# Conditioning sums of the first four k-tiles on TensorE, in a two-layer decoder

## The chip, the cores and the metric

The kernel runs on one core of one Trainium2 chip. The metric is the device time of one execution in microseconds (us). Before the change the median of 3 runs is 2377.34 us (2375.9 to 2378.76). The trace comes from one profiled execution of its own, which took 2369.32 us.

## The reference

Two decoder layers act on x (256 rows of 2048 features, float32). A condition c (2048 numbers) steers every sub-layer through six vectors per layer:

```
c_act = silu(c)
for l in range(2):
    mod = c_act @ w_ada[l] + b_ada[l]            # 2048 x 12288 weights per layer
    sh_a, sc_a, g_a, sh_m, sc_m, g_m = split(mod, 6)
    h = x * (1 + sc_a) + sh_a
    y = mixer(h, w_in[l], ..., w_o[l])           # attention, two kinds of heads
    x = layernorm(ALPHA * x + (1 + g_a) * y)
    h = x * (1 + sc_m) + sh_m
    y = square(relu(h @ w_up[l])) @ w_down[l]
    x = layernorm(ALPHA * x + (1 + g_m) * y)
```

All weights are read once from the chip's memory, as float32: w_ada alone is 2 x 100 MB. The change touches how the first part of `sc_a` and `sh_a` of layer 0 is made.

## The kernel before

The 2048 features lie in 16 k-tiles of 128 partitions. Every dense product splits its float32 operands into a rounded high part and the rest (`wh` and `wl` of the weights, two planes of `hT` for the activations) and multiplies three times: high by high, high by low, low by high (L302 to L304).

Weights stream in blocks of 512 KB into seven buffers with the tag `raw`, all issued from SyncE's queue (SP). A w_in block goes to ScalarE (ACT), which rounds it into `wh` (L134), then to VectorE (DVE), which subtracts to get `wl` (L135), then to TensorE (PE). A w_ada block (`rawa`) takes the same buffers and is summed on VectorE. A buffer is free for the next load when its last reader is done.

For 512 output features, that is four k-tiles, `ada_T` loads 16 blocks, one per k-tile of the condition: 128 rows of w_ada by 512 columns, for the shift vector and the scale vector together (128 x 1024 numbers). For each block VectorE does acc += block x (the condition's column of that k-tile), so that after 16 blocks each partition holds its own part of the sum. TensorE then transposes the eight 128 x 128 squares of `acc` (L166), VectorE adds each one up along its row (L171), adds the bias from `badaT` (L173), and the features lie on partitions in the two tiles called `mod`. Layer 0 begins with four passes over four k-tiles each (`PASSES`), and `first_pass` prepares each. For the first of them nothing else can run beside the sums: TensorE needs `hT`, which needs x transposed (L471) and scaled by the two `mod` tiles on ScalarE (L484), then split on VectorE (L486, L487).

The order of the work on each engine is fixed when the program is built, by the tile framework's scheduler, and an engine runs its list strictly in that order. `side`, `pending` and `later` are lists of work that the code interleaves with weight blocks.

One small place far from the change matters for reading the trace. In `forget`, once per layer, TensorE runs four plain float32 matmuls with 8 moving columns against a stationary tile of 128 columns:

```
for t in range(NT):
    for a in range(2):
        nc.tensor.matmul(pf[:, t * NF:(t + 1) * NF], lhsT=zr[:, a, t * P:(t + 1) * P],
                         rhs=sel[0:2 * NF, :], start=a == 0, stop=a == 1)   # line 715
```

Of the kernel before, what the change touches and what calls it, by code (L numbers as in the profile page):

```python
# [11 lines left out]
F32 = mybir.dt.float32  # L12
# [3 lines left out]
ALU = mybir.AluOpType  # L16
PSUM = bass.MemoryType.PSUM

P = 128
D = 2048  # L20
S = 256
NT = S // P
KT = D // P
# [14 lines left out]
CW = 512  # L38
# [5 lines left out]
RAW_BUFS = 7  # L44
# [29 lines left out]
def decoder(ctx: ExitStack, tc: tile.TileContext, x, c, positions, w_ada, b_ada, w_in, b_f,  # L74
            lambda_q1, lambda_k1, lambda_q2, lambda_k2, subln_g, w_o, ln1_g, ln1_b, w_up, w_down,
            ln2_g, ln2_b, out):
    nc = tc.nc
    const = ctx.enter_context(tc.tile_pool(name="const", bufs=1))
    big = ctx.enter_context(tc.tile_pool(name="big", bufs=1))
    wp = ctx.enter_context(tc.tile_pool(name="wp", bufs=1))  # L80
# [4 lines left out]
    def bank():  # L85
        return psum.tile([P, 512], F32, tag="bank", name="bank", bufs=4)
# [7 lines left out]
    def e1(shape, name, dtype=F32):  # L94
        return sm.tile(shape, dtype, tag="e1", name=name, bufs=E1_BUFS)
# [11 lines left out]
    cact = const.tile([P, KT], F32, name="cact")  # L107
# [8 lines left out]
    badaT = []  # L116

    def bias_T(l):
        r1 = e1([96, P], "r1")
        nc.sync.dma_start(r1, b_ada[l].rearrange("(a p) -> a p", p=P))  # L120
        pv = bank()
        nc.tensor.transpose(pv[:, 0:96], r1, ident[0:96, 0:96])
        bT = const.tile([P, 96], F32, name=f"badaT{l}")
        nc.vector.tensor_copy(bT, pv[:, 0:96])
        badaT.append(bT)


# [15 lines left out]
    def ada_add(acc, raw, kt, fresh):  # L143
        k = cact[:, kt:kt + 1]
        if fresh:
            nc.vector.tensor_scalar(acc, raw, k, None, ALU.mult)
        else:
            nc.vector.scalar_tensor_tensor(acc, raw, k, acc, ALU.mult, ALU.add)  # L148

    def ada_T(l, vec, kt0):  # L150

        acc = gp.tile([P, 2, CW], F32, tag="acc", name="acc", bufs=1)
        for kt in range(KT):
            raw = wp.tile([P, 2, CW], F32, tag="raw", name="rawa", bufs=RAW_BUFS)
            rows = w_ada[l, kt * P:(kt + 1) * P, :].rearrange("p (v n) -> p v n", n=D)
            nc.sync.dma_start(raw, rows[:, vec:vec + 2, kt0 * P:kt0 * P + CW])
            ada_add(acc, raw, kt, kt == 0)
            if kt < KT - 1:
                yield 1

        def finish():
            pss = []
            for i in range(2):
                ps = bank()
                for f in range(4):
                    nc.tensor.transpose(ps[:, f * P:(f + 1) * P], acc[:, i, f * P:(f + 1) * P], ident)  # L166
                pss.append(ps)
            yield
            for i, ps in enumerate(pss):
                red = sm.tile([P, 4], F32, tag="red", name="red")  # L170
                nc.vector.reduce_sum(red, ps.rearrange("p (f k) -> p f k", f=4), axis=mybir.AxisListType.X)  # L171
                s0 = (vec + i) * KT + kt0
                nc.vector.scalar_tensor_tensor(modT[l, vec + i][:, kt0:kt0 + 4], red, float(i),  # L173
                                               badaT[l][:, s0:s0 + 4], ALU.add, ALU.add)

        pending[(l, vec, kt0)] = [0, finish()]
        yield 1

    def ada_G(l, vec):
# [29 lines left out]
    modT = {}  # L209
    gates = {}  # L210
    ready = set()
    pending = {}
    side = []
# [5 lines left out]
    def want_mod(l, vec, kts=range(0, KT, 4)):  # L219
        for v in (vec, vec + 1):  # L220
            if (l, v) not in modT:
                modT[l, v] = const.tile([P, KT], F32, name=f"mod{l}_{v}")
        return [ada_T(l, vec, kt0) for kt0 in kts]

    def side_rate(per_block):
        rate[0] = per_block
# [12 lines left out]
    def side_pop():  # L239
        settle()  # L240
        try:
            return next(side[0])
        except StopIteration:
            side.pop(0)
            return 0
# [8 lines left out]
    def side_flush():  # L254
        while side:
            side_pop()
        settle(*pending)
# [110 lines left out]
    def masks():  # L368
        nc.gpsimd.memset(mhalf, -0.5)
        nc.gpsimd.memset(mask, 0.0)  # L370
        nc.gpsimd.affine_select(out=mask[:, 1, :], in_=mask[:, 1, :], compare_op=ALU.is_ge, fill=BIG,
                                base=0, pattern=[[-1, P]], channel_multiplier=1)
        nc.gpsimd.memset(tri, 1.0)
        nc.gpsimd.affine_select(out=tri[:, 0, :], in_=tri[:, 0, :], compare_op=ALU.is_ge, fill=0.0,
                                base=0, pattern=[[1, P]], channel_multiplier=-1)

        nc.gpsimd.memset(sel, 0.0)

        nc.gpsimd.memset(FL.bitcast(F32), 0.0)
        nc.gpsimd.memset(FG, 0.0)  # L380
        for i in range(4):
            nc.gpsimd.affine_select(out=sel, in_=sel, compare_op=ALU.not_equal, fill=1.0, base=-NF * i,
                                    pattern=[[-1, NF]], channel_multiplier=1)

        nc.gpsimd.memset(rowc, 1.0)
        for i in range(4):
            for base, sign in ((-NF * i, 1), (NF * (i + 1) - 1, -1)):
                nc.gpsimd.affine_select(out=rowc[:, i:i + 1], in_=rowc[:, i:i + 1], compare_op=ALU.is_ge,
                                        fill=0.0, base=base, pattern=[[0, 1]], channel_multiplier=sign)
        nc.gpsimd.affine_select(out=rowc[:, 4:5], in_=rowc[:, 4:5], compare_op=ALU.is_ge, fill=0.0,  # L390
                                base=-2 * NF, pattern=[[0, 1]], channel_multiplier=1)

    def constants():
# [58 lines left out]
        for l in range(DEPTH):  # L452
            nc.vector.tensor_scalar(neglam[:, l:l + 1], neglam[:, l:l + 1], -lambda_init(l), None, ALU.add)
            nc.vector.tensor_scalar(subg[:, l:l + 1], subg[:, l:l + 1], 1.0 - lambda_init(l), None, ALU.mult)
        bias_T(1)


    h_steps = [None, KT, KT]

    def need_h(upto):  # L460

        while h_steps[1] < min(upto, h_steps[2]):
            h_steps[1] = next(h_steps[0])
# [3 lines left out]
    def turn(k2):  # L467
        pt = bank().rearrange("p (a s) -> p a s", a=2)
        for j in range(2):
            for t in range(NT):  # L470
                nc.tensor.transpose(pt[:, j, t * P:(t + 1) * P],  # L471
                                    xacc[:, t, (k2 + j) * P:(k2 + j + 1) * P], ident)
        return pt

    def make_h(hT, A, B, kt0, kt1, coef=None):

        for k2 in range(kt0, kt1, 2):
            if coef is not None and k2 % 4 == 0:
                coef(k2)
            pt = turned.pop(k2) if k2 in turned else turn(k2)  # L480
            h32 = e2([P, 2, S], "h32")
            for j in range(2):
                kt = k2 + j
                nc.scalar.activation(h32[:, j, :], pt[:, j, :], AF.Identity,  # L484
                                     bias=B[:, kt:kt + 1], scale=A[:, kt:kt + 1])
            nc.vector.tensor_copy(hT[:, k2:k2 + 2, 0, :], h32)  # L486
            nc.vector.tensor_sub(hT[:, k2:k2 + 2, 1, :], h32, hT[:, k2:k2 + 2, 0, :].bitcast(F32))  # L487
            yield k2 + 2
# [524 lines left out]
    def x_rows(a, b):  # L1013
        for t in range(NT):
            nc.sync.dma_start(xacc[:, t, a * P:b * P], x[0, t * P:(t + 1) * P, a * P:b * P])
        yield (b - a) / 4

    def alpha_x(t, a, b):
        nc.scalar.mul(xacc[:, t, a * P:b * P], xacc[:, t, a * P:b * P], ALPHA)

    def first_pass(i):
        a, b = PASSES[i]
        if i == 0:
            side.extend(want_mod(0, 0, [a]))
            for _ in range(3):
                side_pop()
            for _ in x_rows(a, b):
                pass
            bias_T(0)
            masks()  # L1030
            for k2 in range(a, b, 2):
                turned[k2] = turn(k2)
        side_flush()
        h_steps[:] = [make_h(hT, modT[0, 1], modT[0, 0], a, b), a, b]
        need_h(a + AHEAD)
        for t in range(NT):
            later.extend([nop, nop, nop, nop, lambda t=t: alpha_x(t, a, b)])
        if i == 0:
            rest = constants()
            for _ in range(12):  # L1040
                later.append(lambda: next(rest, None))
        if i + 1 < len(PASSES):
            n = PASSES[i + 1]
            side.extend([x_rows(*n)] + want_mod(0, 0, [n[0]]))
            side_rate(4.5 * (n[1] - n[0]) / ((12 - SKIP) * (b - a) / 2))
        else:
            side.append(ada_G(0, 2))
            side.extend(want_mod(0, 3))

    for l in range(DEPTH):  # L1050
# [20 lines left out]
        else:  # L1071
            side.append(ada_G(l, 5))
            rows = []
# [30 lines left out]
```

## Time and profile before

| what | value |
|---|---|
| median of 3 runs | 2377.34 us |
| profiled execution | 2369.32 us |
| its span, first to last instruction | 2367.6 us |
| PE busy | 2281.3 us (96%) |
| DVE busy | 1790.1 us (76%) |
| ACT busy | 1155.3 us (49%) |
| moved by DMA | 619.37 MB, mean 262 GB/s |
| third dense matmul starts at | 38.16 us |

Times inside the trace count from the span's start; 1.7 us of the execution lie outside the span. A busy share is an average over stages. PE is nearly idle up to 37 us and nearly full from there on, so the two stretches are read apart. PE is the matmuls, PEld the loads of the stationary operand, which run beside the matmul before. The column of the granted clock reads 1.00 for all stretches before 41.7 us; durations of the rows themselves tell the level there.

### The profile page before, as it was taken

The page shows a single profiled execution, that of the slowest core. Times are in us where ns is not written, and L with a number is a line of the kernel's source. Part 1 is how long each engine was busy: PE and PEld are TensorE (multiplying, and loading weights), DVE is VectorE, ACT ScalarE, POOL GpSimd, SP SyncE. Part 2 cuts the span into 40 slices and gives each one's busy share as a digit, 9 for nine tenths or more (in the row PEclk, how much of TensorE's full clock was granted, in tenths as well). Part 3 has the DMA queues.
Part 4 walks back from the last instruction along what each step waited for, and adds up shares of the span by engine and source line. Part 5 has one row for each costly group of instructions (what it writes and reads, how often), then busy time and mean ns, then how long its engine had stood idle before and what let it go on. Part 6 is the DMA issues. An engine that isn't in the chain of part 4 may idle for free.

```text
span 2367.6 us, 33293 instructions
## 1 busy us (share of the span) xinstructions
PE 2281.3 (96%) x12444; PEld 1959.6 (83%) x12444; DVE 1790.1 (76%) x2339; ACT 1155.3 (49%) x1684; POOL 35.1 (1%) x60
## 2 busy tenths in 40 slices
PE   4999999899999999999999999999999999999998
PEld 3878798699989888888777778987888888888886
DVE  7899888988888778888777975667675666555657
ACT  2543675344546345346444663444554553553542
POOL 0000010000000000000000000000000000000000
PEclk9999999999999999999999999999999999999999
DMA  9999688889898888888759877765777777756653
GB/s 344 326 331 308 193 265 305 312 315 325 303 349 301 302 281 309 312 293 300 273 186 303 292 226 234 233 215 170 221 263 251 229 242 240 230 189 195 187 188 123
DMA packets 309890, 619.37 MB, mean 262 GB/s; under 512 B 24200, under 2 KB 25048, under 8 KB 309728
## 3 DMA queue, kind: packets, MB, share of 16 engines
q1 hardware_dynamic: 309728, 617.25, 77.6%
q8 instruction: 97, 1.59, 0.3%
q14 instruction: 65, 0.53, 0.1%
HBM read 615.07 MB, written 2.10 MB: 261 GB/s over the span
## 4 chain that ended last, share of the span: by engine, by line
PE 76%; DVE 9%; DMA 9%; issue 3%; ACT 2%; POOL 0%; SPq 0%; DVEq 0%; ACTq 0%; POOLq 0%
PE mm L303 13%; PE mm L302 13%; PE mm L304 13%; PE mm L908 7%; PE bank L908 7%; DMA rawa<-in_w_ada_dram 5%; PE mm L331 4%; PE mm L330 4%; PE mm L328 4%; PE mm L910 4%; PE bank L910 4%; DVE wl L135 4%; DVE acc L148 2%; DMA raw<-in_w_in_dram 1%; ACT wh L134 1%
## 5 line engine op out<-in xcount | busy, mean ns | idle before, releaser
L134 ACT CAST wh<-raw 128x1024 fp32r<-128x1024 f32 x752 | 789.5, 1052 | 929.5 <-PE mm L304 491.5
L135 DVE TENSOR_TENSOR wl<-raw,wh 128x1024 fp32r<-128x1024 f32 x752 | 913.7, 1221 | 347.2 <-ACT wh L134 343.9
L148 DVE SCALAR_TENSOR_TENSOR acc<-rawa,cact,acc 128x1024 f32<-128x1024 f32 x368 | 471.0, 1280 | 137.8 <-DMA rawa<-in_w_ada_dram 136.5
L303 PE MATMUL mm<-wl,Hs 128*128 128x512 f32 x992 | 386.5, 390 | 2.0 <-DVE wl L135 1.9
L302 PE MATMUL mm<-wh,Hs 128*128 128x512 f32 x992 | 386.2, 389 | 0.0
L304 PE MATMUL mm<-wh,Hs 128*128 128x512 f32 x992 | 386.0, 389 | 0.0
L331 PE MATMUL mm<-hT,wl 128*128 128x256 f32 x1024 | 289.6, 285 | 6.0 <-DVE wl L135 5.4
L328 PE MATMUL mm<-hT,wh 128*128 128x256 f32 x1024 | 290.9, 285 | 1.9 <-DVE hT L486 1.1
L330 PE MATMUL mm<-hT,wh 128*128 128x256 f32 x1024 | 289.8, 284 | 0.2 <-DVE hT L487 0.2
L908 PE MATMUL mm<-hT,wh 128*128 128x512 f32 x768 | 286.7, 396 | 0.5 <-DVE hT L487 0.5
L908 PE MATMUL bank<-hT,wh 128*128 128x512 f32 x768 | 286.2, 395 | 0.0
L303 PEld LDWEIGHTS mm<-wl,Hs 128*128 128x128 f32 x992 | 186.2, 188 | 41.9 <-DVE wl L135 3.5
L302 PEld LDWEIGHTS mm<-wh,Hs 128*128 128x128 f32 x992 | 186.2, 188 | 38.7
L304 PEld LDWEIGHTS mm<-wh,Hs 128*128 128x128 f32 x992 | 186.2, 188 | 38.6
L910 PE MATMUL mm<-hT,wl 128*128 128x256 f32 x768 | 215.5, 281 | 0.2 <-DVE wl L135 0.2
L910 PE MATMUL bank<-hT,wl 128*128 128x256 f32 x768 | 215.3, 280 | 0.0
L302 PE MATMUL mm<-wh,hT 128*128 128x512 f32 x512 | 200.8, 400 | 5.9 <-DVE hT L486 5.7
L303 PE MATMUL mm<-wl,hT 128*128 128x512 f32 x512 | 203.4, 397 | 3.1 <-DVE wl L135 2.7
L331 PEld LDWEIGHTS mm<-hT,wl 128*128 128x128 f32 x1024 | 196.0, 192 | 8.7 <-DVE wl L135 8.3
L304 PE MATMUL mm<-wh,hT 128*128 128x512 f32 x512 | 200.9, 393 | 0.0
L328 PEld LDWEIGHTS mm<-hT,wh 128*128 128x128 f32 x1024 | 196.8, 192 | 3.4 <-DVE hT L486 1.3
L330 PEld LDWEIGHTS mm<-hT,wh 128*128 128x128 f32 x1024 | 197.1, 192 | 0.8 <-DVE hT L487 0.4
(248 smaller groups left out, 2665.7 us busy)
## 6 DMA issues: line engine op xcount, KB each, us to landing
rawa<-in_w_ada_dram SPq DMA_DIRECT2D x384, 512.0 KB, 5.5
raw<-in_w_up_dram SPq DMA_DIRECT2D x256, 512.0 KB, 4.8
raw<-in_w_down_dram SPq DMA_DIRECT2D x256, 512.0 KB, 5.1
raw<-in_w_in_dram SPq DMA_DIRECT2D x192, 512.0 KB, 5.4
raw<-in_w_o_dram SPq DMA_DIRECT2D x64, 512.0 KB, 4.6
gb<-in_ln_g_dram SPq DMA_DIRECT2D x12, 256.0 KB, 5.5
bb<-in_ln_b_dram SPq DMA_DIRECT2D x12, 256.0 KB, 5.3
xacc<-in_x_dram SPq DMA_DIRECT2D x8, 256.0 KB, 6.7
```

The lines of the kernel that those rows point to most:

```text
L134: nc.scalar.copy(wh, raw)
L135: nc.vector.tensor_sub(wl, raw, wh.bitcast(F32))
L148: nc.vector.scalar_tensor_tensor(acc, raw, k, acc, ALU.mult, ALU.add)
L302: nc.tensor.matmul(o, lhsT=hi, rhs=wh, start=start, stop=False)
L303: nc.tensor.matmul(o, lhsT=hi, rhs=wl, start=False, stop=False)
L304: nc.tensor.matmul(o, lhsT=lo, rhs=wh, start=False, stop=stop)
L328: nc.tensor.matmul(o, lhsT=wh[:, j, cs], rhs=hT[:, kt, 0, :], start=first and kt == kt0 and f % 2 == 0, stop=False)
L330: nc.tensor.matmul(o, lhsT=wh[:, j, cs], rhs=hT[:, kt, 1, :], start=False, stop=False)
L331: nc.tensor.matmul(o, lhsT=wl[:, j, cs], rhs=hT[:, kt, 0, :], start=False, stop=last and kt == kt1 - 1 and f % 2 == 1)
L908: nc.tensor.matmul(pu[f], lhsT=wh[:, j, cs], rhs=hT[:, kt].rearrange("p a s -> p (a s)"), start=kt == kt0, stop=False)
L910: nc.tensor.matmul(pu[f][:, 0:S], lhsT=wl[:, j, cs], rhs=hT[:, kt, 0, :], start=False, stop=kt == kt1 - 1)
```

## The change

A new function `ada_start` takes the place of `ada_T` for the first four k-tiles of layer 0's shift and scale, and for those alone. It loads the same 16 blocks into the same seven buffers. Each 128 x 128 square of a block becomes the stationary operand of a matmul, with one column of the condition (`cact`) as the moving operand; eight such matmuls per block write eight columns of one accumulator bank, and 16 blocks add up there. The features come out on partitions, and VectorE adds the bias straight from the bank. The transposes, the row sums and VectorE's products of this part are gone. The bias is loaded, transposed and copied before the blocks, and its copy moves from VectorE to ScalarE, for both layers.

```diff
@@ bias_T
-        nc.vector.tensor_copy(bT, pv[:, 0:96])
+        nc.scalar.copy(bT, pv[:, 0:96])
@@
+    def ada_start(l, vec, kt0):
+
+        ps = bank()
+        for kt in range(KT):
+            raw = wp.tile([P, 2, CW], F32, tag="raw", name="rawa", bufs=RAW_BUFS)
+            rows = w_ada[l, kt * P:(kt + 1) * P, :].rearrange("p (v n) -> p v n", n=D)
+            nc.sync.dma_start(raw, rows[:, vec:vec + 2, kt0 * P:kt0 * P + CW])
+
+            for i in range(2):
+                for f in range(4):
+                    c = i * 4 + f
+                    nc.tensor.matmul(ps[:, c:c + 1], lhsT=raw[:, i, f * P:(f + 1) * P], rhs=cact[:, kt:kt + 1],
+                                     start=kt == 0 and c == 0, stop=kt == KT - 1 and c == 7)
+            if kt < KT - 1:
+                yield 1
+        for i in range(2):
+            s0 = (vec + i) * KT + kt0
+            nc.vector.scalar_tensor_tensor(modT[l, vec + i][:, kt0:kt0 + 4], ps[:, i * 4:i * 4 + 4], float(i),
+                                           badaT[l][:, s0:s0 + 4], ALU.add, ALU.add)
+        ready.add((l, vec, kt0))
+        yield 1
@@ first_pass
         if i == 0:
-            side.extend(want_mod(0, 0, [a]))
+            bias_T(0)
+            want_mod(0, 0, [])
+            side.append(ada_start(0, 0, a))
             for _ in range(3):
                 side_pop()
             for _ in x_rows(a, b):
                 pass
-            bias_T(0)
             masks()
```

The rows below give the order of instructions on an engine, without times; after the change the line numbers of the later code stand 22 higher (L302 becomes L324).

TensorE at the program's start, before: `ident,r` is the bias, `ident,xacc` are transposes of x, `ident,acc` those of the finished sums.

```order
L106 MATMUL bank<-ident,crow 128x16
L122 MATMUL bank<-ident,r_119 128x96
L471 MATMUL bank<-ident,xacc 128x128 x8
L166 MATMUL bank<-ident,acc 128x128 x8
L302 MATMUL mm<-wh,hT 128x512
L303 MATMUL mm<-wl,hT 128x512
L302 MATMUL mm<-wh,hT 128x512
L304 MATMUL mm<-wh,hT 128x512
```

The same place after the change:

```order
L106 MATMUL bank<-ident,crow 128x16
L122 MATMUL bank<-ident,r_105 128x96
L190 MATMUL bank<-cact,rawa 128x1 x24
L493 MATMUL bank<-ident,xacc 128x128 x8
L190 MATMUL bank<-cact,rawa 128x1 x104
L324 MATMUL mm<-wh,hT 128x512 x2
L325 MATMUL mm<-wl,hT 128x512
L326 MATMUL mm<-wh,hT 128x512
```

128 one-column matmuls (L190) stand on TensorE ahead of the first dense matmul, with x's transposes after the third block; two products with `wh` come before the first one with `wl`.

ScalarE up to the first results, before: `wh` is a w_in block's rounded part, `h` the scaled x, `dv` the first result.

```order
L108 ACTIVATE cact<-bank 128x16
L1019 ACTIVATE xacc<-xacc 128x512 x2
L134 CAST wh<-raw 128x1024 x2
L484 ACTIVATE h_222<-bank,mod_0_105,mod_1_106 128x256 x2
L484 ACTIVATE h_227<-bank,mod_0_105,mod_1_106 128x256 x2
L134 CAST wh<-raw 128x1024 x2
L798 COPY dv_272<-mm 128x512 x2
```

And after:

```order
L108 ACTIVATE cact<-bank 128x16
L124 COPY badaT_109<-bank 128x96
L1041 ACTIVATE xacc<-xacc 128x512 x2
L506 ACTIVATE h_320<-bank,mod_0_111,mod_1_112 128x256 x2
L506 ACTIVATE h_325<-bank,mod_0_111,mod_1_112 128x256 x2
L134 CAST wh<-raw 128x1024 x3
L820 COPY dv_370<-mm 128x512 x2
```

The bias copy came in, and the first two blocks' `wh` casts moved from ahead of the four `h` to behind them.

VectorE over the same stretch, before (`red` are the row sums):

```order
L146 TENSOR_SCALAR acc<-rawa,cact 128x1024
L124 COPY badaT_123<-bank 128x96
L148 SCALAR_TENSOR_TENSOR acc<-rawa,cact,acc 128x1024 x15
L171 TENSOR_REDUCE red<-bank 128x4
L135 TENSOR_TENSOR wl<-raw,wh 128x1024
L173 SCALAR_TENSOR_TENSOR mod_0_105<-red,badaT_123 128x4
L171 TENSOR_REDUCE red<-bank 128x4
L173 SCALAR_TENSOR_TENSOR mod_1_106<-red,badaT_123 128x4
L135 TENSOR_TENSOR wl<-raw,wh 128x1024
L486 CAST hT<-h_222 128x2x256
```

And after:

```order
L196 SCALAR_TENSOR_TENSOR mod_0_111<-bank,badaT_109 128x4
L196 SCALAR_TENSOR_TENSOR mod_1_112<-bank,badaT_109 128x4
L508 CAST hT<-h_320 128x2x256
L509 TENSOR_TENSOR hT<-h_320,hT 128x2x256
L508 CAST hT<-h_325 128x2x256
L509 TENSOR_TENSOR hT<-h_325,hT 128x2x256
L135 TENSOR_TENSOR wl<-raw,wh 128x1024 x2
L146 TENSOR_SCALAR acc<-rawa,cact 128x1024
```

The sixteen products and the bias copy are gone, and the first two `wl` moved from beside the bias adds to behind both pairs of `hT`.

## Rows read from the trace of the kernel before

**Rows 1.** The page: shares of the chain of waits, by engine.

```profile
PE 76%; DVE 9%; DMA 9%; issue 3%; ACT 2%; POOL 0%; SPq 0%; DVEq 0%; ACTq 0%; POOLq 0%
```

**Rows 2.** Waits of PE, 0 to 45 us: us in total, times, longest.

```profile
PE bank L166 <- DVE acc L148: 18.4, 1, 18.4
PE mm L302 <- DVE hT L486: 3.5, 1, 3.5
```

**Rows 3.** The chain in order of time: start, us, what.

```profile
3.93 7.23 DMA r<-in_b_ada_dram
```

**Rows 4.** Timeline of VectorE: start, us, engine, line, operation.

```profile
5.02 0.75 DVE L146 TENSOR_SCALAR acc<-rawa,cact 128x1024 f32<-128x1024 f32 x1 [3.93 <-DMA rawa<-in_w_ada_dram]
11.84 19.77 DVE L148 SCALAR_TENSOR_TENSOR acc<-rawa,cact,acc 128x1024 f32<-128x1024 f32 x15
...
33.48 1.22 DVE L135 TENSOR_TENSOR wl<-raw,wh 128x1024 fp32r<-128x1024 f32 x1
...
35.41 0.16 DVE L173 SCALAR_TENSOR_TENSOR mod<-red,badaT 128x4 f32<-128x4 f32 x1
...
36.66 0.43 DVE L486 CAST hT<-h 128x512 fp32r<-128x512 f32 x1
...
37.66 0.68 DVE L487 TENSOR_TENSOR hT<-h,hT 128x512 fp32r<-128x512 f32 x1
```

**Rows 5.** Timeline of PE, 0 to 39 us.

```profile
11.42 1.91 PE L471 MATMUL bank<-ident,xacc 128*128 128x128 f32 x8
31.75 1.94 PE L166 MATMUL bank<-ident,acc 128*128 128x128 f32 x8 [18.42 <-DVE acc L148]
37.14 0.79 PE L302 MATMUL mm<-wh,hT 128*128 128x512 f32 x1 [3.45 <-DVE hT L486]
...
38.16 0.63 PE L302 MATMUL mm<-wh,hT 128*128 128x512 f32 x1
```

**Rows 6.** Windows: engines' busy us (x instructions), granted clock, DMA share, GB/s.

```profile
11.84:31.70 19.86, 1.49 (x7) 1.09 (x6) 19.26 (x16) 2.19 (x3) 0.00 (x0) 1.00 1.05 389
...
41.70:97.00 55.30, 54.84 (x297) 47.41 (x295) 45.28 (x72) 29.63 (x41) 0.00 (x0) 1.00 0.98 336
```

**Rows 7.** Timeline of SP: issues of DMAs.

```profile
3.93 0.64 SPq L120 DMA_DIRECT2D r<-in_b_ada_dram  x1
```

**Rows 8.** Line 715, 230 to 236 us: duration ns min/median/max.

```profile
L715 PEld LDWEIGHTS bank<-sel,zr x8: 181/187/187, 234.1 to 234.9; 16*128 16x128 f32 x8
```

**Rows 9.** Timeline of PEld, the weight loads, at three places.

```profile
37.14 0.29 PEld L302 LDWEIGHTS mm<-wh,hT 128*128 128x128 f32 x1 [3.85 <-DVE hT L486]
...
234.14 0.96 PEld L715 LDWEIGHTS bank<-sel,zr 16*128 16x128 f32 x8 [0.35 <-issue]
235.12 0.19 PEld L302 LDWEIGHTS mm<-wh,hT 128*128 128x128 f32 x1
```

**Rows 10.** Windows where the granted clock changed; columns as in rows 6.

```profile
260.20:263.60 3.40, 2.47 (x12) 1.47 (x11) 3.40 (x9) 2.81 (x7) 0.00 (x0) 1.00 0.48 143
263.61:267.00 3.39, 3.39 (x9) 2.60 (x9) 3.38 (x20) 0.99 (x4) 0.00 (x0) 0.50 0.54 169
...
475.90:478.60 2.70, 2.69 (x13) 2.67 (x14) 2.30 (x7) 1.75 (x4) 0.00 (x0) 0.50 0.61 194
478.70:482.00 3.30, 3.30 (x29) 3.17 (x28) 3.29 (x9) 1.75 (x5) 0.00 (x0) 1.00 0.03 7
```

**Rows 11.** Timeline of PE within the half-clock stretch, and before it.

```profile
261.47 1.62 PE L648 MATMUL bank<-dkT,dqT 64*128 64x128 f32 x8
...
264.32 0.63 PE L304 MATMUL mm<-wh,hT 128*128 128x512 f32 x1
```

**Rows 12.** Timeline of ScalarE, 0 to 45 us.

```profile
13.15 1.15 ACT L1019 ACTIVATE xacc<-xacc 128x512 f32<-128x512 f32 x2 [10.11 <-PE bank L471]
30.39 1.04 ACT L134 CAST wh<-raw 128x1024 fp32r<-128x1024 f32 x1 [16.09 <-DMA raw<-in_w_in_dram]
...
35.61 1.93 ACT L484 ACTIVATE h<-bank,mod,mod 128x256 f32<-128x256 f32 x4 [1.46 <-DVE mod L173]
```

## The prediction

> **What bounds the kernel now.** I read the chain of waits first. TensorE holds 76% of it, VectorE and DMA 9% each [rows 1]; by place, PE is nearly full from 41.7 us on (54.84 of 55.30 us busy up to 97 us) [rows 6]. So what moves the start of the dense matmuls moves the end by about as much, unless work behind it has slack to give back.
>
> Then the waits of PE in the first 45 us. One wait of 18.4 us ends with VectorE's last product for `acc`, and one of 3.5 us with `hT` [rows 2]. Before the first, the chain goes through the bias: its DMA was issued behind three w_ada blocks and x, took 7.23 us and landed at 11.16 [rows 3]. Its copy stood on VectorE between the first product (5.02) and the other fifteen, which run from 11.84 for 19.77 us [rows 4], 1.32 us each. Over that stretch DMA delivers 389 GB/s [rows 6], which is 1.35 us for a block of 512 KB. Loads and VectorE are thus nearly in step. The reader is to see that two things pace this start, and that taking VectorE away leaves the loads: there is little to win beyond the late begin at 11.84.
>
> After the sums come eight transposes at 31.75 (1.94 us), row sums, and the second `mod` tile at 35.41 + 0.16 = 35.57. From there `h` takes 1.93 us on ScalarE for four [rows 12], `hT` follows, and the dense matmuls start at 37.14, the third at 38.16 [rows 5]. I use this third one as the marker, since it is the first that needs `wl` after the change.
>
> **The change part by part.** Removed: sixteen products on VectorE (0.75 + 19.77 us), eight transposes, two row sums. All stood on the path. VectorE has nothing else to do there, so their worth is only the path's.
>
> Added: 128 matmuls with one moving column, each with its own 128 x 128 float32 stationary square. The price is that of the loads of the stationary operand. The nearest rows are line 715: 8 moving columns, 128 stationary columns, plain float32. The code has four matmuls there per layer and the trace shows eight loads, so one such matmul runs as two records. The eight take 0.96 us, the last alone 0.187 [rows 8, 9], so one follows the other after (0.96 - 0.187) / 7 = 0.110 us. For 128 matmuls that makes 256 records, 28.3 us at this spacing; a block costs 16 x 0.110 = 1.77 us, more than VectorE's 1.32 or the load's 1.35. So PE, not the loads, would pace the start.
>
> That holds at full clock. At the start PE is not there: the third dense matmul lasts 0.63 us [rows 5], exactly as one at 264.32 [rows 11] in a stretch where the granted clock reads 0.50 [rows 10], the 1.2 GHz level. A first load took 0.29 us at 37.14 and 0.19 at 235.12 [rows 9], 0.10 more at the half level. I take 0.11 + 0.10 = 0.21 us per record there. The low bound for the half level is 0.11 (the load doesn't care), the high one 0.29 (each load stands alone, nothing overlaps). I choose 0.21, since the two loads differ only in the level.
>
> Does the stream of one-column matmuls lift the clock? No row shows one that long. What rows show: the clock rose just before 478.7 behind 14 loads and transposes that kept PE busy for 2.69 us. It fell at 263.6, behind a stretch in which PE was busy 2.47 of 3.40 us [rows 10], much of it eight matmuls on 64 of the 128 rows [rows 11]. So it has fallen behind work that occupied PE most of the time, and a one-column matmul sends less through the array than any row here. I take the half level for the whole stream, and keep the full level as a rival.
>
> The sum, on the trace's clock. The bias DMA now goes ahead of the blocks; its issue takes 0.64 us [rows 7], so the first block is usable at 5.02 + 0.64 = 5.66. Three blocks, 48 records: 10.1 us, to 15.7. Eight transposes of x queue behind them, 1.91 us [rows 5], to 17.6; x has landed by then, as the next blocks have. Thirteen blocks, 208 records: 43.7 us, to 61.3. Two bias adds of 0.16 us and the hand-over: `mod` at 61.7.
>
> Then an order that hurts. On ScalarE the `wh` casts now stand behind the four `h`, and on VectorE the `wl` behind both `hT` pairs. In the old order a `wh` cast was done at 31.4 [rows 12], long before. From `mod`: the first `hT` cast at +1.09 (36.66 - 35.57), then 0.43 + 0.68 twice, +3.3; `wh` is ready at 1.97 + 1.05 = +3.0; `wl` takes 1.22, +4.5 [rows 4, 12]. The third dense matmul starts at +4.55, against 38.16 - 35.57 = +2.59 before. That is 2 us lost, whatever the stream costs. Third matmul: 61.7 + 4.55 = 66.25, less 38.16 makes +28.1 us.
>
> Costed at nothing: the bias copy on ScalarE, which sat idle for 10.11 us there [rows 12] (about 0.3 us if that cover were gone); the slower loads while PE paces them, for the w_in blocks behind them land while PE is still loading squares. The seven buffers are now freed by PE, at 3.4 us per block, so DMA drops to some 156 GB/s in that stretch; it is not given back later, since at most seven blocks can wait ready. VectorE's freed 20 us lie where it would idle. The dense matmuls begin at the half level as before, so nothing there changes.
>
> The profiled execution, 2369.32 us, becomes 2397.4. The median of the runs shown lies 8 us higher; on that base I forecast 2377.3 + 28.1 = 2405.4 us.
>
> **The rivals.** First, the stream lifts the clock, and the change comes out even. For: PE is occupied without a gap, as in the 14 transposes that raised it. Then about 5 us run at the half level (24 records), 232 records at 0.110 take 25.6 us, the transposes some 1 us: end at 5.66 + 5 + 25.6 + 1 = 37.3, `mod` at 37.7, third matmul at 42.3, +4.1. The dense matmuls now start at full clock, which saves half of the 4.6 us up to 41.7 that ran at the half level, 2.3: +1.8 us, 2379.2. This is the other side, not slower: it decides if full clock is granted by about 12 us. The Trainium skill (TensorE: Matmul & The Clock Gate, Part 1) has the gate set by how busy the engine has recently been; by that rule as it stands this rival would hold. The fall at 263.6 with PE busy 2.47 of 3.40 us does not fit it well.
>
> Second, a load keeps its 0.11 us at either level. Then the end is 5.66 + 28.3 + 1.9 = 35.9, `mod` 36.3, third matmul 40.8: +2.7, 2380.0. For it speaks that line 715's spacing may be the feeding of instructions; against it the 0.29 beside the 0.19. The skill's same page (LDWEIGHTS) prices a load at its columns over 1.2 GHz, 107 ns for 128, and names no level: the 0.110 at full clock agrees, the 0.29 does not, and by the page the 256 records would cost 27.3 us, an estimate.
>
> Third, faster: with one column instead of eight a record costs less than 1.35 / 16 = 0.085 us, and the loads pace the start. The last block lands at about 5.66 + 15 x 1.35 + 1.35 for x = 27.3; with `mod` near 28.6 and the 4.55 behind it the third matmul starts at 33.2, -5.0 us: 2372.4, or 2370 if the clock is up too. Against: a record's load has 128 columns however few move.
>
> Fourth, worse: at the half level load and matmul don't overlap, 0.29 per record, 256 x 0.08 = 20 us on top: 2426.
>
> **How the numbers follow.** Forecast 0.61, first rival 0.19, second 0.08, third 0.08, fourth 0.04. The forecast's own range is 2400 to 2412: 3 us for the spacing (0.20 to 0.22) and 3 for the order behind `mod` and the drift of the base. The whole range takes in the first two rivals, 2376 to 2412; the third and fourth, about 0.12, lie outside. About 0.2%, 4.8 us, is what a measurement of this kernel can tell from no change. The first two rivals lie inside it except for their tails: same 0.26; faster 0.09 from the third; slower 0.65.
>
> **What would show it.** In the changed profile the one-column matmuls (line 190) should come as 256 records from about 5.7 us, spaced 0.21 us, ending near 61, with the first full granted clock only after the dense matmuls have run some 4 us. PE's wait for VectorE's `acc` is gone; the third dense matmul waits for `wl` near 66 us; the rest of the trace is the old one, moved by 28 us. Spacing of 0.11 after the first 5 us means the first rival, 0.11 from the first record the second, waits on w_ada loads between the blocks the third, 0.29 the fourth. I am also wrong if the later passes, which wait for sums that VectorE still makes, give back several us.

## The result and the profile after

The changed kernel takes 2401.33 us (median of 4 runs, 2397.56 to 2407.11), the kernel before in the same sitting 2376.62 us (4 runs, 2374.53 to 2378.76). The ratio is 1.0114 [1.0082, 1.0146]: slower by 19 to 35 us. The profiled execution is the one of 2407.11 us, with a span of 2405.4.

The chain of waits, shares by engine, looks the same as in [rows 1], with DMA and VectorE in the other order:

```profile
PE 76%; DMA 9%; DVE 9%; issue 3%; ACT 2%; POOL 0%; DVEq 0%; SPq 0%; ACTq 0%; POOLq 0%
```

A total over 2400 us hides a change in the first 60. The line of the one-column matmuls shows it: duration in ns (min/median/max), first and last start in us.

```profile
L190 PEld LDWEIGHTS bank<-cact,rawa x256: 289/333/338, 5.5 to 61.4; 128*128 128x128 f32 x128
L190 PE MATMUL bank<-cact,rawa x256: 212/352/353, 5.5 to 61.5; 128*128 128x1 f32 x128
```

The 128 matmuls run as 256 records (rows of the trace), and the shortest load lasts 289 ns. [rows 9] showed both prices of a first load, 0.29 us before the clock came up and 0.19 at full clock; here not one of 256 shows the lower. The timeline of PE answers [rows 5]: start and length in us, operation, count, and in brackets the wait ahead.

```profile
5.51 10.38 PE L190 MATMUL bank<-cact,rawa 128*128 128x1 f32 x48 [1.90 <-DMA rawa<-in_w_ada_dram]
15.75 1.95 PE L493 MATMUL bank<-ident,xacc 128*128 128x128 f32 x8
17.49 44.37 PE L190 MATMUL bank<-cact,rawa 128*128 128x1 f32 x208
65.17 1.22 PE L324 MATMUL mm<-wh,hT 128*128 128x512 f32 x2 [3.31 <-ACT wh L134]
66.71 0.79 PE L325 MATMUL mm<-wl,hT 128*128 128x512 f32 x1 [0.32 <-DVE wl L135]
...
71.14 0.63 PE L324 MATMUL mm<-wh,hT 128*128 128x512 f32 x1
...
72.12 0.39 PE L324 MATMUL mm<-wh,hT 128*128 128x512 f32 x1
```

208 records in 44.37 us is 0.213 us each, nearly twice the 0.110 worked out from [rows 8, 9]. PE waits for nothing from 17.49 to 61.86. The dense matmuls drop from 0.63 to 0.39 us only at about 71.6: up to there PE is at the 1.2 GHz level. The third dense matmul starts at 66.71 against 38.16: its offset, how much later than before it starts, is 28.55 us.

VectorE and ScalarE after the sums, to set beside [rows 4, 12]:

```profile
61.98 0.23 DVE L196 SCALAR_TENSOR_TENSOR mod<-bank,badaT 128x4 f32<-128x4 f32 x2 [60.89 <-PE bank L190]
...
64.82 0.69 DVE L509 TENSOR_TENSOR hT<-h,hT 128x512 fp32r<-128x512 f32 x1
65.43 2.35 DVE L135 TENSOR_TENSOR wl<-raw,wh 128x1024 fp32r<-128x1024 f32 x2
```

```profile
62.25 1.93 ACT L506 ACTIVATE h<-bank,mod,mod 128x256 f32<-128x256 f32 x4 [43.58 <-DVE mod L196]
64.06 2.94 ACT L134 CAST wh<-raw 128x1024 fp32r<-128x1024 f32 x3
```

`mod` is there at 62.21 and the third dense matmul 4.50 us later; it was 2.59 before. The casts stand behind the four `h`, so the first dense wait is for ScalarE's `wh` (3.31 us), and `wl` comes behind both `hT` pairs.

Two windows of the stream (columns as in [rows 6]), one early and one after the buffers were full:

```profile
6.00:16.00 10.00, 10.00 (x49) 10.00 (x49) 0.00 (x0) 0.00 (x0) 0.00 (x0) 1.00 1.01 353
20.00:41.00 21.00, 21.00 (x100) 21.00 (x100) 0.00 (x0) 0.00 (x0) 0.00 (x0) 1.00 0.48 151
```

PE is busy for all of both stretches, and DMA falls from 353 to 151 GB/s once PE, which frees the buffers, sets the pace. The granted-clock column reads 1.00 until the first change that was recorded; the level is told here by the loads, none shorter than 0.289 us, and by the dense matmuls of 0.63 us behind them.

Two more us arise later. VectorE's small operations on positions stand among the `wl` there, and PE waits:

```profile
96.26 0.61 PE L324 MATMUL mm<-wh,hT 128*128 128x512 f32 x2
97.16 0.50 PE L325 MATMUL mm<-wl,hT 128*128 128x512 f32 x1 [0.29 <-DVE wl L135]
...
99.58 0.61 PE L324 MATMUL mm<-wh,hT 128*128 128x512 f32 x2
101.15 0.50 PE L325 MATMUL mm<-wl,hT 128*128 128x512 f32 x1 [0.96 <-DVE wl L135]
```

In the kernel before no `wl` is waited for there, though the same operations stand among its `wl` from 62 to 70 us. What differs as well is ScalarE's order. Before, four `wh` casts stand ahead of the first two copies of results (`dv`), after the change three, so the fourth cast comes behind copies that wait for PE. The first two rows are from the kernel before, the others from the changed one:

```profile
42.36 1.05 ACT L134 CAST wh<-raw 128x1024 fp32r<-128x1024 f32 x1 [3.89 <-PE mm L304]
44.36 0.59 ACT L798 COPY dv<-mm 128x512 f32<-128x512 f32 x1 [0.95 <-PE mm L304]
...
73.70 1.27 ACT L820 COPY dv<-mm 128x512 f32<-128x512 f32 x2 [6.70 <-PE mm L326]
74.86 2.00 ACT L134 CAST wh<-raw 128x1024 fp32r<-128x1024 f32 x2
```

The fourth cast starts 32.5 us later than before, where PE's matmuls are 29.4 later. The second marker, the first `hT` matmul of the next pass, is at 129.13 against 97.59: +31.5 us. From there to 260 us the offset stays within 0.1 us; further on it grows, with steps back of 1 to 2 us, to 37.8 at the end.

### The profile page after: what moved, and what is told of

Read it like the earlier page. It is cut to its first block, busy times and chain, and to the rows that moved or that the text cites. A ratio compares the mean times of both kernels' runs of the same rounds, so it can differ in the third digit from the quotient of the medians.

```text
span 2405.4 us, 33757 instructions
## 1 busy us (share of the span) xinstructions
PE 2338.9 (97%) x12692; PEld 2015.0 (84%) x12692; DVE 1769.2 (74%) x2319; ACT 1155.3 (48%) x1686; POOL 35.3 (1%) x60
## 4 chain that ended last, share of the span: by engine, by line
PE 76%; DMA 9%; DVE 9%; issue 3%; ACT 2%; POOL 0%; DVEq 0%; SPq 0%; ACTq 0%; POOLq 0%
PE mm L325 13%; PE mm L326 13%; PE mm L324 13%; PE mm L930 7%; PE bank L930 7%; DMA rawa<-in_w_ada_dram 6%; PE mm L353 4%; PE mm L350 4%; PE mm L352 4%; DVE wl L135 4%; PE mm L932 3%; PE bank L932 3%; PE bank L190 2%; DVE acc L148 2%; ACT wh L134 1%
## 5 line engine op out<-in xcount | busy, mean ns | idle before, releaser
L148 DVE SCALAR_TENSOR_TENSOR acc<-rawa,cact,acc 128x1024 f32<-128x1024 f32 x353 | 451.8, 1280 | 157.0 <-DMA rawa<-in_w_ada_dram 156.0
L324 PE MATMUL mm<-wh,Hs 128*128 128x512 f32 x992 | 386.2, 389 | 0.0
L324 PEld LDWEIGHTS mm<-wh,Hs 128*128 128x128 f32 x992 | 186.2, 188 | 38.8
L324 PE MATMUL mm<-wh,hT 128*128 128x512 f32 x512 | 200.1, 402 | 5.6 <-ACT wh L134 3.3
```

The lines of the kernel that those rows point to most:

```text
L324: nc.tensor.matmul(o, lhsT=hi, rhs=wh, start=start, stop=False)
```

## The experiments

Two measures recur: the third dense matmul ("third", 38.16 before, 66.71 after) and the start of the next pass ("pass", 97.59 and 129.13). The kernel before had a median of 2373.26 us (20 runs) beside the first four experiments, 2372.28 (29 runs) beside the next four, and ranged from 2366.82 to 2379.93. Edits are against the changed kernel, save for experiment 2.

**1. The changed kernel again.** No edit; is the loss of the first 66 us kept to the end?

> The changed kernel once more, unedited, in five rounds, to size the change. My theory (256 records at the half level, 2 us of order behind the bias adds, 2 us of VectorE's lag) says the shift is made before 105 us and carried whole: +24 to +32 us over the kernel before, third dense matmul again near 66.7 us. If the later stages give time back (rival), the traced offset against the kernel before shrinks after 250 us and the median shows under +22.

2402.14 us (2400.58 to 2407.88), ratio 1.0122 [1.0101, 1.0143], +24 to +34 us. Pass is at 128.92, and at 2302 us of the before trace the same matmuls are 31.2 us late. Between, the offset went up to 35 and back. Nothing is given back; the two profiled executions of one kernel differ by 6.5 us at the end (2400.58, 2407.11), so a later offset of that size is no effect of the change.

**2. Only the move of the bias.** The kernel before, with its sums on VectorE; the bias is loaded and turned first.

```diff
-        nc.vector.tensor_copy(bT, pv[:, 0:96])
+        nc.scalar.copy(bT, pv[:, 0:96])
...
+            bias_T(0)
             side.extend(want_mod(0, 0, [a]))
...
-            bias_T(0)
```

> The kernel before with one part of the change alone: the bias is loaded, transposed and copied (on ScalarE) ahead of the blocks; the sums stay on VectorE. Theory: VectorE's fifteen products no longer wait for the copy from 5.8 to 11.8 us and follow the loads, the last block landing near 28; the sums end near 29 to 30 instead of 31.6 and the third dense matmul starts 2 to 3 us earlier, at 35 to 36: 2374 us, 0.1% faster, hardly to be told from no change. Rival, that the loads and not the copy already set the end: third matmul at 38, no difference in the trace.

2373.92 us, ratio 1.0003 [0.9989, 1.0017]. Third is at 36.78, 1.4 us earlier where 2 to 3 were expected, because VectorE no longer waits for the bias but for a block that was queued behind x:

```profile
12.68 1.28 DVE L148 SCALAR_TENSOR_TENSOR acc<-rawa,cact,acc 128x1024 f32<-128x1024 f32 x1 [2.72 <-DMA rawa<-in_w_ada_dram]
```

So the move of the bias costs nothing that shows, and the loss belongs to the sums on PE and to the order that the program has with them. It also shows how little VectorE could have freed: without its late begin, the loads are next.

**3. 64 moving columns.** The condition's column is repeated 64 times by a stride of zero: the same loads, more columns behind each.

```diff
-                    nc.tensor.matmul(ps[:, c:c + 1], lhsT=raw[:, i, f * P:(f + 1) * P], rhs=cact[:, kt:kt + 1],
+                    nc.tensor.matmul(ps[:, c * 64:c * 64 + 64], lhsT=raw[:, i, f * P:(f + 1) * P],
+                                     rhs=cact[:, kt:kt + 1].broadcast_to([P, 64]),
...
```

> The changed kernel with the condition's column repeated 64 times as the moving operand: the same 256 loads of stationary squares, 64 columns through the array for each instead of 1. Theory, that the cost is the half clock and one column does not lift it: the granted clock rises within some 10 us of the stream's start, spacing falls from 0.21 to 0.11 us, the stream ends near 37 instead of 61.9, the third dense matmul starts near 42: 2376 to 2381 us, within 0.2% of before. Rival, that the spacing is the load's and the feeding's own price: spacing stays at 0.21, end near 62, 2400 us as after the change.

The nine times fall into two groups: 2377.11, 2381.52, 2385.43, 2385.53 and 2399.57, 2399.79, 2402.91, 2403.52, 2408.25. A median (2399.57, ratio 1.0089 [1.0058, 1.012]) says little of such a pair. The traced execution was of the first group:

```profile
20.00:41.00 21.00, 21.00 (x191) 21.00 (x190) 0.00 (x0) 0.00 (x0) 0.00 (x0) 1.00 0.84 276
```

190 loads in 21 us are 0.110 each, against 100 in the same window of after. The rate changed at 19.3 us, just behind x's eight transposes; third is 46.78, where 42 was expected. What the other group does was seen later (9 and 10).

**4. Casts ahead.** One column; the first two blocks of w_in are loaded and split before the last four w_ada blocks, so that `wh` and `wl` don't stand behind `h` and `hT`.

```diff
+            if kt == KT - 4:
+                for kb in (0, 2):
+                    ahead.append(wload(rows_of(w_in[0])(kb, 2, OFF_DV, CW), 2, CW))
...
```

> The changed kernel with the first two w_in blocks loaded before the last four w_ada blocks, so that their splits (wh on ScalarE, wl on VectorE) stand ahead of the scaled x on both engines. Theory: the third dense matmul starts 2.4 to 2.6 us behind the bias adds instead of 4.5, and VectorE, two wl earlier, no longer makes TensorE wait near 97 and 101 us (1.25 us there): 3 to 4 us less than after the change, about +21 to +25 over the kernel before. Rival, that the order costs nothing because VectorE's lag moves elsewhere: the offset at 105 us stays at 31 us.

2399.0 us (2396.07 to 2401.67), ratio 1.0104 [1.0083, 1.0124], +20 to +29 us. The first and third dense matmul:

```profile
63.78 0.79 PE L331 MATMUL mm<-wh,hT 128*128 128x512 f32 x1 [1.84 <-DVE hT L515]
...
64.80 0.63 PE L331 MATMUL mm<-wh,hT 128*128 128x512 f32 x1
```

Third is 1.9 us earlier than in the first trace of the changed kernel, 2.6 behind `mod`, as in the kernel before; pass is 126.22, 2.7 earlier than in experiment 1. So the order behind `mod` cost about 2 us; the other 26.6 us of third's offset stand with the stream. The expectation that the later waits for `wl` go with it was wrong: 1.2 us of them stay, and ScalarE still has three casts ahead of the first copies.

**5. 128 moving columns.** As 3, with 128 columns and two banks.

```diff
-        ps = bank()
+        ps = [bank(), bank()]
...
-                    nc.tensor.matmul(ps[:, c:c + 1], lhsT=raw[:, i, f * P:(f + 1) * P], rhs=cact[:, kt:kt + 1],
+                    nc.tensor.matmul(ps[i][:, f * P:(f + 1) * P], lhsT=raw[:, i, f * P:(f + 1) * P],
+                                     rhs=cact[:, kt:kt + 1].broadcast_to([P, P]),
...
```

> The changed kernel with the condition's column repeated 128 times (two accumulator banks). With 64 columns the clock rose in some executions, right behind the transposes of x, and in others the time was that of one column. Theory: with 128 columns the stream lifts the clock by itself in every execution, by some 13 us; spacing 0.21 before and 0.11 after; stream ends at 37 to 39, third dense matmul at 42 to 44; the time is 2377 to 2383 us in all executions. Rival, that it was the transposes alone that lifted it: the rise comes only behind them, at about 19 us, or not at all, and the times fall in two groups again.

2376.45 us (10 runs, 2369.78 to 2379.66, one group, its median just below the 2377 to 2383 expected), ratio 1.0009 [0.9998, 1.002]. Three stretches of the stream:

```profile
5.80:11.00 5.20, 5.20 (x24) 5.20 (x25) 0.00 (x0) 0.00 (x0) 0.00 (x0) 1.00 0.98 291
11.30:13.80 2.50, 2.50 (x24) 2.50 (x24) 0.00 (x0) 0.00 (x0) 0.00 (x0) 1.00 1.04 393
14.80:37.80 23.00, 23.00 (x208) 23.00 (x207) 3.45 (x7) 3.22 (x4) 0.00 (x0) 1.00 1.00 350
```

25 loads in 5.20 us, then 24 in 2.50: the level changed near 11.2 us, ahead of any transpose of x, and stayed to the stream's end. This is the change with nothing taken off PE's work (columns were added to every matmul), and nearly all of the loss is gone. What is left shows at the end of the stream:

```profile
14.69 23.39 PE L190 MATMUL bank<-cact,rawa 128*128 128x128 f32 x208
42.63 0.80 PE L326 MATMUL mm<-wh,hT 128*128 128x512 f32 x1 [4.56 <-DVE hT L510]
...
43.66 0.63 PE L326 MATMUL mm<-wh,hT 128*128 128x512 f32 x1
```

PE waits 4.56 us, the dense matmuls are back at the half level (0.63), and third is 5.5 us later than before. In VectorE's order position operations and a `wl` stand ahead of the two bias adds or between them (39.55 and 40.89, where the sums ended at 38.1). ScalarE has four casts ahead of the first copies here, and PE has none of the later waits for `wl`.

**6. A warm start.** One column as in the changed kernel, behind 16 matmuls of ones, 512 columns each, that count for nothing in the output.

```diff
+            warm = mm()
+            for n in range(16):
+                nc.tensor.matmul(warm, lhsT=ones_r, rhs=ones_r.unsqueeze(1).broadcast_to([P, 4, P]),
+                                 start=n == 0, stop=n == 15)
             bias_T(0)
```

> The changed kernel with 16 matmuls of 512 columns (ones times ones, result unused) ahead of the stream, so that it begins at full clock; the stream starts near 8.7 us instead of 5.5. Theory, that one column does not hold the clock: after at most a few us at 0.11 the spacing goes to 0.21 and stays; end at 60 to 64, third dense matmul at 65 to 68, 2398 to 2404 us. Rival, that one column can hold what it cannot raise: spacing 0.11 throughout, end near 38, third matmul near 43, 2378 us.

2405.84 us (2403.08 to 2412.38), 2 us above the range expected, ratio 1.0144 [1.0128, 1.0161]. The stream begins at 7.88 us, at full clock:

```profile
7.90:9.50 1.60, 1.60 (x15) 1.60 (x15) 0.00 (x0) 0.21 (x1) 0.00 (x0) 1.00 1.01 257
9.70:15.00 5.30, 5.30 (x27) 5.30 (x26) 0.00 (x0) 0.00 (x0) 0.00 (x0) 0.50 1.03 381
20.00:60.00 40.00, 40.00 (x190) 40.00 (x189) 0.00 (x0) 0.00 (x0) 0.00 (x0) 0.50 0.49 158
```

This is the clearest row of the study. The same instruction goes at 0.11 us per load up to 9.5 and at 0.20 behind the recorded fall of the granted clock at 9.6, and DMA delivers more in the second stretch than in the first, so the squares (the 128 x 128 weights) were not late. And PE is busy 40.00 of 40.00 us at a granted 0.50. The stream does not merely fail to raise the clock, it lets it fall.

**7. 128 columns and casts ahead,** the edits of 4 and 5 together.

> 128 columns and the first two w_in blocks' splits ahead, both remedies on the changed kernel: stream's end as with 128 columns alone, third dense matmul 2 us earlier, at 40 to 42, no waits of TensorE for wl near 75 us: 2374 to 2379 us, not told from the kernel before. If it stays at or above 2381 us, there is a third cost that I have not named.

2377.35 us (12 runs), ratio 1.0016 [1.0006, 1.0027], not told from experiment 5 (1.0009 [0.9998, 1.002]). Against the kernel before it is slower by 1.4 to 6.4 us, where no difference was expected. Third is 42.35, 1.3 us earlier than in 5, just behind the 40 to 42 expected: a third `wl` still stands ahead of the bias adds at 39.53. As in 5, four casts stand ahead of the first copies and PE has none of the later waits for `wl`, though the operations on positions do stand among the `wl` here; pass is 102.52 against 103.92.

**8. Half and half.** VectorE sums the shift half of each block, PE the scale half with 128 columns; the bias first.

```diff
...
+                nc.vector.scalar_tensor_tensor(acc, raw[:, 0, :], cact[:, kt:kt + 1], acc, ALU.mult, ALU.add)
+            for f in range(4):
+                nc.tensor.matmul(ps[:, f * P:(f + 1) * P], lhsT=raw[:, 1, f * P:(f + 1) * P],
+                                 rhs=cact[:, kt:kt + 1].broadcast_to([P, P]),
...
```

> A version meant to beat both: of each w_ada block VectorE sums the shift half (512 columns, about 0.65 us) while TensorE sums the scale half with 128 repeated columns (0.9 us at full clock), both under the 1.35 us that a block's load takes; bias first. Theory, loads now pace the start: last block near 28, bias adds done near 30.5, third dense matmul at 33 to 34 instead of 38.2, of which the bias-first run suggests that a third is lost again in the first pass: 2368 to 2372 us, 0.1 to 0.3% faster. Rival, that the first pass is bound by loads and VectorE anyway: the traced offset shrinks to under 2 us by 105 us and the time is that of before.

2369.76 us (12 runs, 2367.41 to 2373.78), ratio 0.999 [0.9981, 0.9999]: the best of the study, 0.2 to 4.5 us faster than the kernel before and so only just told from no change. PE near the end of the sums:

```profile
29.92 1.16 PE L193 MATMUL bank<-cact,rawa 128*128 128x128 f32 x8 [0.20 <-DMA rawa<-in_w_ada_dram]
...
34.01 0.50 PE L335 MATMUL mm<-wh,hT 128*128 128x512 f32 x1 [2.50 <-DVE hT L519]
...
34.58 0.40 PE L335 MATMUL mm<-wh,hT 128*128 128x512 f32 x1
```

PE now waits for each block's load, as VectorE does. Third is 3.6 us earlier than before (34.58, where 33 to 34 was expected). With both engines waiting for loads, a faster sum on the same loads has little more to win. By pass (96.12) 1.5 us are left of it, since the waits for `wl` of 1.2 us come here too (three casts ahead of the first copies).

**9 and 10. 64 columns, two more executions** of kernel 3, unedited.

> 64 repeated columns once more, for a trace of the other group of times. Theory: where the time is near 2400 us the granted clock has not risen behind the transposes of x, the spacing is 0.21 us to the stream's end near 62 us; where it is near 2380 us the rise is at 16 to 20 us and the spacing 0.11 behind it. Rival: both groups have the same start, and the 20 us between them come later.

> The same as the run before, a third trace: either group, with the spacing of its group.

2411.29 and 2406.28 us, one run each (the kernel before beside them 2369.35). Both are of the second group. In experiment 9:

```profile
20.00:41.00 21.00, 21.00 (x101) 21.00 (x100) 0.00 (x0) 0.00 (x0) 0.00 (x0) 1.00 0.47 150
```

100 loads where the traced execution of 3 had 190, in the same window of the same program; the rate never changed, and in experiment 10 neither (208 records in 44.48 us in both). So, as far as these three traces show, the two groups of times are with and without the rise of the clock.

## Why the prediction was right

The forecast was slower, 2405.4 us or +28.1; 2401.33 was measured, +24.7, and +28.9 in experiment 1. Some of that closeness is luck, since the trace has +31.5 by the second pass. Each step against its row:

- **The price of a load, 0.21 us at the half level.** 0.213 measured. The 0.10 by which a lone load lasts longer at the half level was added to the spacing at full clock, which no row had tested; twice the spacing, 0.22, fits nearly as well, so it is partly luck. The bounds, 0.11 and 0.29, are both out as a spacing; 0.29 to 0.33 is what a load record lasts, but two of them overlap. The second rival (0.11 at either level) and the fourth (0.29) fall with it. Experiment 6 shows both prices in one stream. The Trainium skill (TensorE: Matmul & The Clock Gate, LDWEIGHTS) puts a load at its columns over 1.2 GHz, 107 ns for 128 as an estimate: that fits the full level (23.39 / 208 = 0.112 us in experiment 5) and not the half level.
- **The stream leaves the clock at the half level.** It does, for all of 56 us, and experiment 6 shows it lets a full clock go. The argument, that one column sends little through the array, is borne out in direction: more columns behind the same loads brought the clock up, sometimes with 64 and in every run with 128 as far as times and traces show. The Trainium skill (the same page, Part 1) sets the gate by how busy the engine has recently been. By the row at a granted 0.50 with PE busy 40.00 of 40.00 us, busy as the profile counts it is not what decides here. The first rival, at 0.19, falls. Its price was about right where its condition was made to hold: it put the third dense matmul at 42.3 and experiment 5 has 43.66. It is luck in part: the second bias add came 3.3 us later than that rival had it, at 41.04, and third stood 2.6 behind it in place of 4.55. It had the dense matmuls start at full clock, and they started at the half level, behind a wait of 4.56 us.
- **The start and the end of the stream.** First block 5.66 forecast, 5.51 measured; end 61.3 and 61.86; `mod` 61.7 and 62.21. The half microsecond is about what 208 records at 3 ns more come to.
- **The order behind `mod`.** +4.55 forecast, +4.50 measured; experiment 4 takes 1.9 us of it back by moving the casts alone.
- **The loads.** 156 GB/s forecast while PE paces them, 151 measured, and PE waits for no w_in block's load right behind it. The third rival, loads pacing the start, needs less than 0.085 us per record, and no row of any run shows that with 16 per block. With half the squares on PE, in experiment 8, it does hold.
- **What was costed at nothing and was not.** "The dense matmuls begin at the half level as before, so nothing there changes" failed: they stay there for 6.4 us (65.17 to 71.6) instead of 4.6, and the offset grows from 28.55 to 29.4. The two waits for `wl` follow, and it is 31.5 behind them. "The rest of the trace is the old one, moved by 28 us" should have read 31.5. These 3 us are within what the later stages wander by from one execution to the next, so the time could not tell; only the trace does.

Why `wl` is late near 97 us after the change and not before is read from the traces, not tested by itself. The kernels with four casts ahead of the first copies (before and experiments 2, 5 and 7) have neither wait; those with three (the changed kernel, 3, 4, 6, 8, and so 1, 9 and 10) have both. The operations on positions alone don't explain it, for they stand among the `wl` in the kernel before and in 2 and 7 as well. No run moved that one cast alone. The prediction had this order in its rows and gave it no price. What in a stream brings the clock up is also open: the runs show which streams did, and 64 columns did and did not.

## What to carry to other kernels

A product with one column pays for the load of its whole stationary square: 16 loads of a 512 KB block took 3.41 us at the half level and 1.8 at the full one, where VectorE needed 1.32 and the block's own load 1.35, so with one column such a sum is worth moving to TensorE only where PE idles anyway and nothing waits for the end. Half of it, with the column repeated, made the best run here. Price it at the clock that holds at that place, read from durations of known instructions, since the granted-clock column may show its first recorded change late. Before taking an engine off a path, look what paces beside it: here the loads stood at 1.35 us a block, and the best split won 3.6 us at its place and 0.2 to 4.5 at the end. And when an order of work moves, count what stands ahead of what on every engine: one cast behind two copies goes with the 2 us of waits near 97 us.

## What the runs showed of the hardware

- TensorE can lose its clock while the profile shows it busy without a gap: in experiment 6 the granted clock fell from full to half 1.7 us into the one-column stream and stayed there for 61 us, until the dense matmuls had begun.
- Added work made a stream faster. With 128 columns in place of one, the same 208 records took 23.39 us in place of 44.37. At full clock the extra columns cost next to nothing: 0.112 us a record (experiment 5) against 0.107 with one column (experiment 6, 15 records in 1.60 us).
- One program can have two groups of times that go with the clock: 64 columns gave 2377 to 2386 us in four executions and 2399 to 2412 in seven; the clock rose at 19.3 us in the one traced of the first group and not within the stream in the two of the second.
- At the half level 64 columns cost nothing beside one: 208 records in 44.48 us against 44.37.
